# Hymba-style decoder layer on one core: start bytes of the split weights and of the activation blocks in SBUF

## The chip, the core and the metric

One NeuronCore of one Trainium2 chip runs the whole layer in one launch. The metric is device time in microseconds of that core, from runs of the whole program. Five engines work side by side: TensorE (PE: matmuls, with the weight loads listed apart as PEld), VectorE (DVE), ScalarE (ACT), GpSimd (POOL) and SyncE (SP, which here only issues DMAs). Data lies in SBUF, a memory of 128 partitions; each tile is a stretch of bytes at the same place in every partition, so one start byte says where it is. Matmul results go to PSUM.

## The reference

One decoder layer over 16 meta tokens and 512 tokens, width 2048, hidden width 5632, in float32. `l` is the only layer.

```python
h = jnp.concatenate([meta, x], axis=1)
n = _rmsnorm(h, g_mix[l])
q, k, v, gb, gc, u = jnp.split(n @ w_in[l], ...)
o_attn = _stick_breaking_attention(norm(q), norm(k), v)   # 8 heads of 128
o_conv = gb * _causal_dwconv(gc * u, conv_w[l])           # 1024 channels
o = jnp.concatenate([_rmsnorm(o_attn, g_attn_out[l]), _rmsnorm(o_conv, g_conv_out[l])], axis=-1)
h = h + o @ w_out[l]
n2 = _rmsnorm(h, g_ffn[l])
h = h + (jax.nn.silu(n2 @ w_gate[l]) * (n2 @ w_up[l])) @ w_down[l]
return h[:, N_META:]
```

## The kernel before

**Precision.** TensorE multiplies in a float32 form of lower precision (`F32R`). To keep float32 accuracy every operand is split in two: `hi` is the value rounded to `F32R` (a copy on ScalarE), `lo` the rest (a subtraction on VectorE). A product is three matmuls per tile of 128 rows: weight hi × activation hi, weight hi × activation lo, weight lo × activation hi.

**Stages.** The input projections and attention heads come first, then the short convolution (`pc`, `pu`, `pb` are its products; its activations are the tiles `nh` and `nl`, its weights `whi` and `wlo`), then the output projection, which works with `wide_product` on 512 columns. These use the helper at lines 161 to 173 or lines 639 to 648. From about 850 us on the feed-forward part runs: 44 pairs of gate and up products, then, over four chunks of the hidden width, 32 pairs of down products. Nearly all of its time is in `pair_product` (line 663).

**A pair.** `pair_product` multiplies a 2 × 2 arrangement of weight quarters with a 2 × 2 arrangement of activation halves with seven block products instead of eight. Seven activation blocks, `acts[0]` to `acts[6]`, stand against seven weight combinations, formed from the four loaded quarters `b11`, `b12`, `b21`, `b22` by sums on VectorE (`t1`, `t2`, `t3`, line 598). `block_product` (line 650) runs one of the seven: for each weight tile `k` of 128 columns the three matmuls at lines 659, 660 and 661, each of 128 × 128 weights with 256 activation columns. A block has 24 matmuls in a gate/up pair (8 weight tiles), and 15 or 18 in a down pair (5 or 6). Results gather in the PSUM banks `x`, `y`, `z`.

**The split weights.** `split_quad` (line 588) writes hi and lo of one weight combination into one tile of tag `s`, hi first, lo 4096 bytes behind it; ScalarE writes hi (line 591), VectorE lo (line 592). There are three such buffers, taken in turn. `prepare_ahead` keeps two combinations ahead of TensorE. As a pair takes seven of the three buffers' turns, every activation block meets each of the three in turn from pair to pair. The same buffers serve the output projection before (30 splits).

**The activation blocks.** `slot` (line 699) allocates a tile a little larger than the block and returns a view that starts 16 bytes in: hi and lo of `n` tiles of 256 columns, each tile 1024 bytes. In the gate/up stage the seven are `f0` to `f6`, which stay for the whole stage. In the down stage twelve tiles `r0` to `r11` form a ring: `load_acts` (line 845) loads the seven blocks of the next chunk into the next free ones from DRAM, by DMAs that GpSimd issues (line 851), while the chunk before is multiplied.

**Where the tiles lie.** Pools are stacks, so a tile's start follows from the sizes of those allocated before it. Modulo 128, in bytes, for the view that TensorE reads:

| | start byte modulo 128 |
|---|---|
| split weights, all three buffers, hi and lo | 96 |
| `f0`, `f2`, `f5` | 112 |
| `f1`, `f3`, `f4`, `f6` | 48 |
| ring tiles `r0`, `r2`, `r4`, `r7`, `r9`, `r11` | 112 |
| ring tiles `r1`, `r3`, `r5`, `r6`, `r8`, `r10` | 48 |
| `whi` and `wlo` of the convolution stage | 96 |
| `nh` as read by `pc` and `pu` (two halves of 258 columns) | 16 and 24 |
| `nl` as read by `pc` and `pu` | 80 and 88 |

The steps inside a block (1024 bytes from tile to tile of the activations, 512 of the weights, whole kilobytes from hi to lo) keep these remainders.

Of the kernel before, what the change touches and what calls it, by code (L numbers as in the profile page):

```python
# [10 lines left out]
F32R = mybir.dt.float32r  # L11
# [4 lines left out]
P = 128  # L16
# [9 lines left out]
T2 = SEQ // 2  # L26
# [6 lines left out]
def hybrid_layer(ctx: ExitStack, tc: tile.TileContext, xT, w_in, w_out, w_gu, w_down, vecs, out):  # L33
# [12 lines left out]
    def open_pool(name, bufs=1, **kw):  # L46
        return tc.alloc_tile_pool(name=name, bufs=bufs, reuse_waits="tile", **kw)
# [501 lines left out]
    sw = open_pool("sw", side="right")  # L549
# [12 lines left out]
    quads, sums, split_w, used = {}, {}, [], [0]  # L562
    S_AHEAD = 2
# [22 lines left out]
            load_quad(0, q)  # L586

    def split_quad(src, n):
        t = sw.tile([P, 2, 8 * P], F32R, tag="s", bufs=S_AHEAD + 1, name=f"s{len(split_w)}")
        hi, lo = (t[:, i, : n * P] for i in range(2))  # L590
        sc.copy(hi, src)  # L591
        ve.tensor_tensor(lo, src, hi.bitcast(F32), ALU.subtract)  # L592
        split_w.append((hi, lo))
# [6 lines left out]
    def prepare_pair():  # L600
        if len(split_w) < WIDE:
            with tc.high_priority():
                split_quad(wide[len(split_w)], 8)
                load_wide()
            return
# [4 lines left out]
        with tc.high_priority():  # L610
            b = {q: quads[i, q] for q in ("11", "12", "21", "22") if (i, q) in quads}
            if s == 0:
                split_quad(b["11"], n)
                add_quads(i, "t1", b["11"], b["12"])
                load_quad(i + 1, "11")
            elif s == 1:
                split_quad(sums["t1"], n)
                add_quads(i, "t2", sums["t1"], b["22"])
                add_quads(i, "t3", b["12"], b["22"])
                load_quad(i + 1, "12")  # L620
            elif s == 2:
                split_quad(sums["t2"], n)
            elif s == 3:
                split_quad(b["22"], n)
                load_quad(i + 1, "22")
            elif s == 4:
                split_quad(sums["t3"], n)
            elif s == 5:
                split_quad(b["21"], n)
                ve.tensor_tensor(sums["t2"], sums["t2"], b["21"], ALU.add)  # L630
                load_quad(i + 1, "21")
            else:
                split_quad(sums["t2"], n)
# [64 lines left out]

    def slot(pool, dt, n, tag, name):

        t = pool.tile([P, 2 * n * T2 + 16], dt, tag=tag, name=name)
        return t[:, 4 : 4 + 2 * n * T2].rearrange("p (a k t) -> p a k t", a=2, k=n)

    def pad(pool):
        pool.tile([P, 8], F32, name=f"pad_{pool.name}")

    acts = [slot(fpool, F32R, 8, f"f{i}", f"f{i}") for i in range(4)]
    fx = [dram.tile([P, 2, 8, T2], F32R, name=f"fx{s}") for s in range(4, 7)]
    for _ in range(4):
# [12 lines left out]
    for i, j in enumerate(OUT_TILES):  # L722
# [8 lines left out]
        half, k = divmod(j, 8)  # L731
# [22 lines left out]
        if i == KT - 1:  # L754
# [10 lines left out]
            def ring_tile(dt, name):  # L765
                i = n_ring[0] % 12
                n_ring[0] += 1
                return slot(rings_p[0 if i == 0 else 1 if i < 6 else 2], dt, 6, f"r{i}", name)

            r0 = ring_tile(F32R, "r0_0")  # L770
            fpool_last = open_pool("fpool_last")
            acts += [slot(fpool_last, F32R, 8, f"f{s}", f"f{s}") for s in range(4, 7)]
            for s in range(3):
                n = 7 if s else 8
# [40 lines left out]
    at = [(c, k) for c, n in enumerate(CHUNKS) for k in range(n)]  # L815
# [156 lines left out]
```

## Time and profile before

| | us |
|---|---|
| median of three runs | 2156.65 |
| the three runs | 2154.67 to 2163.67 |
| the profiled execution | 2159.77 |
| its span, first to last instruction | 2157.9 |

The granted TensorE clock over the span is 0.996 of full speed. In the profile an engine's line gives busy time, share of the span and the number of instructions. A matmul's duration runs from its start to its end, and matmuls overlap, so the time that a row of them takes is seen in the distance of their starts, or in how many start in a window. Rows of groups name line, engine, operation, output from inputs (buffer numbers left out), shape and count; then busy us and mean ns of one, then the idle time before them. Names in the profile leave numbers out: `f` stands for all of `f0` to `f6`, `s` for all three buffers, `r` for the ring.

### The profile page before, as it was taken

What the parts mean: (1) busy time and instruction counts of PE and PEld (TensorE: products, weight loads), DVE (VectorE), ACT (ScalarE), POOL (GpSimd) and SP (SyncE); (2) the same over time, 40 slices, a digit from 0 to 9 for tenths busy, and PEclk for the clock granted to TensorE, in tenths of its full rate; (3) what the DMA queues carried; (4) which work ended last, traced back from release to release, by engine and by line L of the source; (5) the groups of instructions that cost most, each with busy time, mean ns of one, the idle gap of its engine ahead of it and who ended that gap; (6) DMA issues with size and microseconds to landing.
All of it is one profiled execution on the core that took longest, in us unless ns stands there. A gap on an engine that the chain in (4) does not pass through costs nothing.

```text
span 2157.9 us, 39367 instructions
## 1 busy us (share of the span) xinstructions
PE 2118.5 (98%) x16086; PEld 2038.7 (94%) x16086; DVE 1645.9 (76%) x2137; ACT 1018.6 (47%) x1576; POOL 451.2 (21%) x579
## 2 busy tenths in 40 slices
PE   8999999999999998999999999999999899999999
PEld 7999999999988878999999999999999899999999
DVE  8777777433347677888888889889888677777798
ACT  6666565322224334454455445445544444444443
POOL 4111111101014541221211211212101323121222
PEclk9999999999999999999999999999999999999999
DMA  5222222222236656556555654655555999788863
GB/s 169 79 79 79 79 69 79 88 97 89 94 122 186 185 158 204 170 171 179 176 167 152 186 158 149 185 160 156 163 152 159 283 262 298 172 235 232 232 184 114
DMA packets 145941, 342.48 MB, mean 159 GB/s; under 512 B 13392, under 2 KB 58960, under 8 KB 145760
## 3 DMA queue, kind: packets, MB, share of 16 engines
q1 hardware_dynamic: 67680, 214.07, 31.6%
q0 software_dynamic: 78080, 125.89, 21.4%
q8 instruction: 126, 2.06, 0.4%
q14 instruction: 55, 0.45, 0.1%
HBM read 268.60 MB, written 71.30 MB: 158 GB/s over the span
## 4 chain that ended last, share of the span: by engine, by line
PE 90%; DMA 4%; DVE 3%; issue 1%; ACT 1%; POOL 1%; SPq 0%; DVEq 0%; POOLq 0%; ACTq 0%
PE x L659 11%; PE x L660 11%; PE x L661 11%; PE z L659 5%; PE z L660 5%; PE z L661 5%; PE y L661 3%; PE y L659 3%; PE y L660 3%; DMA b<-w_down 2%; PE po L645 2%; PE po L647 2%; PE po L646 2%; PE pv L166 1%; PE pu L170 1%; PE pc L170 1%
## 5 line engine op out<-in xcount | busy, mean ns | idle before, releaser
L591 ACT CAST s<-t 128x1024 fp32r<-128x1024 f32 (+2 forms) x304 | 285.5, 939 | 426.4 <-PE z L661 145.7
L592 DVE TENSOR_TENSOR s<-t,s 128x1024 fp32r<-128x1024 f32 (+2 forms) x304 | 343.7, 1130 | 114.8 <-ACT s L591 114.0
L659 PE MATMUL x<-f,s 128*128 128x256 f32 x1408 | 396.1, 281 | 3.4 <-DVE u L686 3.4
L660 PE MATMUL x<-f,s 128*128 128x256 f32 x1408 | 395.6, 281 | 0.0
L661 PE MATMUL x<-f,s 128*128 128x256 f32 x1408 | 395.3, 281 | 0.0
L591 ACT CAST s<-b 128x1024 fp32r<-128x1024 f32 (+2 forms) x228 | 214.0, 939 | 253.6 <-PE x L661 243.1
L659 PEld LDWEIGHTS x<-f,s 128*128 128x128 f32 x1408 | 266.7, 189 | 3.9 <-DVE u L686 3.6
L660 PEld LDWEIGHTS x<-f,s 128*128 128x128 f32 x1408 | 266.7, 189 | 0.0
L661 PEld LDWEIGHTS x<-f,s 128*128 128x128 f32 x1408 | 266.5, 189 | 0.0
L592 DVE TENSOR_TENSOR s<-b,s 128x1024 fp32r<-128x1024 f32 (+2 forms) x228 | 247.6, 1086 | 7.9 <-ACT s L591 5.9
L135 DVE TENSOR_TENSOR wlo<-raw,whi 128x512 fp32r<-128x512 f32 (+1 forms) x198 | 142.3, 720 | 130.9 <-ACT whi L134 130.3
L823 POOL DMA_DIRECT2D fd<-s x154 | 107.0, 890 | 643.7 <-DVE s L181 641.5
L134 ACT CAST whi<-raw 128x512 fp32r<-128x512 f32 (+1 forms) x198 | 121.3, 614 | 185.3 <-PE pu L168 65.5
L659 PE MATMUL x<-r,s 128*128 128x256 f32 x704 | 199.1, 283 | 9.4 <-DVE d L686 4.2
L659 PE MATMUL z<-f,s 128*128 128x256 f32 x704 | 199.0, 283 | 4.2 <-DVE w L739 2.2
L660 PE MATMUL z<-f,s 128*128 128x256 f32 x704 | 198.9, 283 | 2.4 <-DVE f L181 2.4
L660 PE MATMUL x<-r,s 128*128 128x256 f32 x704 | 198.3, 282 | 2.7 <-DMA r<-fd 2.7
L661 PE MATMUL z<-f,s 128*128 128x256 f32 x704 | 198.7, 282 | 0.0
L661 PE MATMUL x<-r,s 128*128 128x256 f32 x704 | 198.0, 281 | 0.4 <-DVE s L592 0.4
L598 DVE TENSOR_TENSOR t<-b,b 128x1024 f32<-128x1024 f32 (+2 forms) x152 | 164.7, 1083 | 27.5 <-DMA b<-w_down 19.9
L659 PEld LDWEIGHTS x<-r,s 128*128 128x128 f32 x704 | 133.1, 189 | 11.6 <-issue 6.7
L659 PEld LDWEIGHTS z<-f,s 128*128 128x128 f32 x704 | 133.0, 189 | 5.4 <-issue 2.3
(326 smaller groups left out, 5603.7 us busy)
## 6 DMA issues: line engine op xcount, KB each, us to landing
b<-w_gu SPq DMA_DIRECT2D x176, 512.0 KB, 3.5
raw<-w_in SPq DMA_DIRECT2D x92, 512.0 KB, 3.3
fd<-s POOLq DMA_DIRECT2D x154, 256.0 KB, 5.2
b<-w_down SPq DMA_DIRECT2D x64, 384.0 KB, 4.0
r<-fd POOLq DMA_DIRECT2D x28, 768.0 KB, 11.9
b<-w_down SPq DMA_DIRECT2D x64, 320.0 KB, 4.6
r<-fd POOLq DMA_DIRECT2D x28, 640.0 KB, 10.8
wide<-w_out SPq DMA_DIRECT2D x30, 512.0 KB, 3.9
```

Source lines behind the costliest of these rows:

```text
L134: sc.copy(hi[:, :c], raw)
L135: ve.tensor_tensor(lo[:, :c], raw, hi[:, :c].bitcast(F32), ALU.subtract)
L170: pe.matmul(ps, wl, ah[:, a:b], start=False, stop=k == last)
L591: sc.copy(hi, src)
L592: ve.tensor_tensor(lo, src, hi.bitcast(F32), ALU.subtract)
L598: ve.tensor_tensor(sums[name], a, b, ALU.add)
L645: pe.matmul(ps, hi[:, kk], ah, start=k == 0, stop=False)
L646: pe.matmul(ps, hi[:, kk], al, start=False, stop=False)
L659: pe.matmul(ps, hi[:, kk], act[:, 0, k], start=start and k == 0, stop=False, skip_group_check=not start)
L660: pe.matmul(ps, hi[:, kk], act[:, 1, k], start=False, stop=False, skip_group_check=not start)
L661: pe.matmul(ps, lo[:, kk], act[:, 0, k], start=False, stop=k == n - 1, skip_group_check=not start)
L823: gp.dma_start(fd[c][s][:, :, k], t[:, :, i])
```

## The change

Two allocations change. A split-weight tile is 128 bytes longer, and its view starts 32, 48 or 80 bytes in (8, 12 or 20 elements of 4 bytes), by the number of the split modulo 3, that is by buffer. An activation slot is 64 bytes longer than before, and its view starts 0, 16, 32, 48, 80, 96 or 112 bytes in, by the number in its tag modulo 7; so each of `f0` to `f6` has an offset of its own, and the twelve ring tiles go through the list once and start it again.

```diff
     def split_quad(src, n):
-        t = sw.tile([P, 2, 8 * P], F32R, tag="s", bufs=S_AHEAD + 1, name=f"s{len(split_w)}")
-        hi, lo = (t[:, i, : n * P] for i in range(2))
+        t = sw.tile([P, 16 * P + 32], F32R, tag="s", bufs=S_AHEAD + 1, name=f"s{len(split_w)}")
+        at = (8, 12, 20)[len(split_w) % 3]
+        hi, lo = (t[:, at + i * 8 * P :][:, : n * P] for i in range(2))
         sc.copy(hi, src)
         ve.tensor_tensor(lo, src, hi.bitcast(F32), ALU.subtract)
...
     def slot(pool, dt, n, tag, name):
 
-        t = pool.tile([P, 2 * n * T2 + 16], dt, tag=tag, name=name)
-        return t[:, 4 : 4 + 2 * n * T2].rearrange("p (a k t) -> p a k t", a=2, k=n)
+        t = pool.tile([P, 2 * n * T2 + 32], dt, tag=tag, name=name)
+        at = (0, 4, 8, 12, 20, 24, 28)[int(tag[1:]) % 7]
+        return t[:, at : at + 2 * n * T2].rearrange("p (a k t) -> p a k t", a=2, k=n)
```

With the new sizes every slot and every split tile starts at 96 modulo 128, so the views start here:

| | start byte modulo 128 |
|---|---|
| split weights, the three buffers | 0, 16, 48 |
| `f0` to `f6` | 96, 112, 0, 16, 48, 64, 80 |
| `r0` to `r6` | 96, 112, 0, 16, 48, 64, 80 |
| `r7` to `r11` | 96, 112, 0, 16, 48 |

The instructions of every engine and their order stay as they are. Tiles around the slots move by some hundred bytes and keep their remainder modulo 128, but for `d1` and `d2` of the down stage, which go from 32 to 96.

## The prediction

> **What bounds the kernel now.** I read the page first, then the whole run in stretches of 100 us, then single activation blocks, then the waits of TensorE.
>
> ```profile
> span 2157.9 us, 39367 instructions
> PE 2118.5 (98%) x16086; PEld 2038.7 (94%) x16086; DVE 1645.9 (76%) x2137; ACT 1018.6 (47%) x1576; POOL 451.2 (21%) x579
> PEclk9999999999999999999999999999999999999999
> PE 90%; DMA 4%; DVE 3%; issue 1%; ACT 1%; POOL 1%; SPq 0%; DVEq 0%; POOLq 0%; ACTq 0%
> ```
>
> TensorE carries 90% of the chain that ends last, at full granted clock. So the time is a number of matmuls times the step from one start to the next, and an address can matter only by that step or by making another engine late enough to stop TensorE.
>
> ```profile
> 900.00:1000.00 100.00, 100.00 (x847) 99.84 (x846) 89.09 (x97) 49.75 (x65) 21.56 (x28) 1.00 0.58 170
> ...
> 1500.00:1600.00 100.00, 100.00 (x849) 100.00 (x848) 87.74 (x99) 49.63 (x66) 13.16 (x19) 1.00 0.54 156
> ```
>
> Columns: busy us and count of TensorE, weight loads, VectorE, ScalarE, GpSimd; granted clock; DMA share; GB/s. In the gate/up stage 847 matmuls of 256 columns start in 100 us, 118.0 ns apart, and TensorE never stops. Now one gate/up pair, cut at the starts of its seven blocks f0 to f6 (24 matmuls each; the bracketed count includes matmuls that reach over an edge, so divide the length by 24):
>
> ```profile
> 1295.78:1298.63 2.85, 2.85 (x27) 1.00 0.29 101
> 1298.63:1301.50 2.87, 2.87 (x27) 1.00 0.25 93
> 1301.50:1304.22 2.72, 2.72 (x26) 1.00 0.60 191
> 1304.22:1307.08 2.86, 2.86 (x26) 1.00 0.03 7
> 1307.08:1309.92 2.84, 2.84 (x27) 1.00 0.64 125
> 1309.92:1312.77 2.85, 2.85 (x26) 1.00 1.09 310
> 1312.77:1315.63 2.86, 2.86 (x26) 1.00 1.28 390
> ```
>
> Same work seven times, but f2 takes 2.72 us (113.3 ns a matmul) and the other six 17.13 us together (119.0 ns). TensorE waits for nothing in either, and DMA goes from 7 to 390 GB/s without an effect. Longer steps show inside the matmuls:
>
> ```profile
> L660 PE MATMUL x<-f,s 128*128 128x256 f32 x7 | 1.9, 276 | 0.0
> L660 PE MATMUL z<-f,s 128*128 128x256 f32 x8 | 2.3, 282 | 0.0
> ```
>
> The first row is f2, the second f3 beside it: 6 ns longer for the same shape. So something slows the matmul itself by some 5 ns in most blocks and by nothing in a few. That is what operand addresses could change.
>
> **Which addresses.** While a matmul streams its block, the weights of the next one are loaded; I compare the two start bytes modulo 128. Before the change weights always start at 96. Blocks start at 112 (f0, f2, f5: the same 64-byte half as the weights, "near") or 48 (f1, f3, f4, f6: the other half, "far"). From the windows above, near is (2.85 + 2.72 + 2.85) / 72 = 116.9 ns, far (2.87 + 2.86 + 2.84 + 2.86) / 96 = 119.1 ns. Another stage, whose weights also start at 96, has activations at 16 and 24 (nh, far) or 80 and 88 (nl, near):
>
> ```profile
> L166 PE MATMUL pc<-nh,whi 128*128 128x258 f32 x256 | 51.7, 284 | 0.0
> L168 PE MATMUL pc<-nl,whi 128*128 128x258 f32 x256 | 51.5, 282 | 0.0
> ```
>
> Near is again 2 ns shorter, with other tiles and offsets. But near does not make a block free: f0 and f5 cost nearly what far blocks cost. In the down stage two ring tiles that both start at 112 differ too, and each repeats itself:
>
> ```profile
> 1969.26:1970.96 1.70, 1.70 (x18) 1.00 0.66 175
> 1981.68:1983.38 1.70, 1.70 (x18) 1.00 0.85 228
> 2064.03:2066.17 2.14, 2.14 (x20) 1.00 0.51 191
> 2078.99:2081.13 2.14, 2.14 (x21) 1.00 0.50 187
> ```
>
> 15 matmuls in 1.70 us are 113.3 ns, 18 in 2.14 us are 118.9 ns, with the same start modulo 128. So near blocks have at least two rhythms, a free one and a slow one, and which one a block falls into is settled by something that the start byte alone does not tell. No far block of the pair runs free.
>
> **The change, part by part.**
>
> *Instructions.* None is added, removed or reordered on any engine; one GpSimd load of h_over waits for one semaphore less. Term: 0.
>
> *Near and far shares.* There are 11,088 matmuls of 256 columns (44 gate/up pairs × 7 blocks × 24, and 16 down pairs each × 7 × 15 and × 7 × 18). Before, 3 of 7 blocks and 6 of 12 ring tiles are near: 5,040. After, weights start at 0, 16 or 48 in turn and blocks at 96, 112, 0, 16, 48, 64, 80. I call a difference (block minus weights, modulo 128) of 96, 112, 0 or 16 near, since 112, 120 and 16 are near by the rows above, and 32 to 80 far, since 48, 56 and 80 are; the edges at 96, 0, 32 and 64 are an assumption. Counted over all matmuls, 5,608 are then near. 568 more × 2.2 ns (119.1 − 116.9) = −1.2 us. If only the absolute half decides, 5,041 are in the weights' half and the term is 0. I take −1.2.
>
> *Rhythm.* Addresses move by other amounts than 128 bytes too, so each block may fall into another rhythm. f2 gains 24 × (119.0 − 113.3) = 0.137 us a pair, 6.0 us over 44 pairs. Losing that with nothing in its place costs +6.0 us. All near blocks in the free rhythm: f2's 1,056 are so already, the other 4,552 × 5.7 ns = −25.9 us. I take 0, the same share as now, since nothing tells which block locks where.
>
> *Weights 16 bytes off a 32-byte border.* After, two of three split buffers start at 16 or 48; before, all at 96. No weight load of the trace does that. Below: 0, as with activations: f blocks (off by 16) cost 118.0 ns on average. Above: the nearest worse alignment, the halves that start at 24 and 88, 8 bytes off:
>
> ```profile
> 439.78 0.40 PE L168 MATMUL pu<-nl,whi 128*128 128x258 f32 x2
> ...
> 442.19 0.28 PE L170 MATMUL pu<-nh,wlo 128*128 128x258 f32 x1
> ```
>
> 20 matmuls, half of them 8 bytes off, in 2.41 us: 120.5 ns, against 118.0 plus 0.8 for two more columns. That is 1.7 ns on average, 3.4 ns if the odd half bears it. On two thirds of 11,088, 7,392 × 3.4 = +25 us. I take 0, since an offset of 16 is nearer to the blocks that have it than to an offset of 8.
>
> *Writers.* ScalarE and VectorE write the split weights at the new offsets. They already write f blocks 16 bytes off and st tiles on the border:
>
> ```profile
> L180 ACT CAST f<-src 128x256 fp32r<-128x256 f32 x34 | 12.2, 399 | 4.0 <-DVE src L751 3.1 <-DVE src L749 0.9
> L180 ACT CAST st<-src 128x256 fp32r<-128x256 f32 x8 | 3.2, 402 | 0.0
> ```
>
> 399 against 402 ns on ScalarE; on VectorE, in a stretch without GpSimd work,
>
> ```profile
> L181 DVE TENSOR_TENSOR f<-src,f 128x256 fp32r<-128x256 f32 x3 | 1.1, 413 | 0.0
> L181 DVE TENSOR_TENSOR st<-src,st 128x256 fp32r<-128x256 f32 x8 | 3.3, 414 | 0.0
> ```
>
> No difference: 0. The cover would matter if I am wrong, for VectorE is 89% busy in the gate/up stage, with 11 us spare in 100.
>
> *Ring loads.* They land at other offsets. TensorE's waits for them in the down stage:
>
> ```profile
> PE x L660 <- DMA r<-fd: 2.7, 3, 1.3
> PE x L659 <- DMA r<-fd: 1.9, 2, 1.6
> PE z L660 <- DMA r<-fd: 1.6, 1, 1.6
> PE y L659 <- DMA r<-fd: 0.4, 1, 0.4
> PE z L659 <- DMA r<-fd: 0.2, 1, 0.2
> ```
>
> 6.8 us in all, the most that could go; doubled, +6.8. I take 0, as the bytes are the same.
>
> *Sum.* The profiled execution took 2159.77 us, 1.87 around its span of 2157.9; 2159.77 − 1.2 = 2158.6. The median of the runs is 2156.65, 3.1 below that execution, so the forecast is 2155.4, written 2155.
>
> The trace has the same shape at 276 and 282 ns without a wait. The Trainium skill (SBUF — State Buffer, "Who interferes with whom") says that on the engine side only the port pair of VectorE and GpSimd causes contention and that TensorE and ScalarE never wait on anyone. By that rule no offset moves the time; 276 against 282 ns speaks against it, though not which partner it is. By the rule the sum would be 2157, by the rows 2155.
>
> **The rivals.**
>
> *The offsets change nothing.* The two rhythms come from when a block starts, not from where it lies. For it: r tiles with one start byte at 113.3 and 118.9. Against it: f2 and the 258-column rows. Time: 2157.
>
> *More blocks run free.* Now some 1 in 5 near matmuls does (f2's 1,056 of 5,040). If weights and blocks at many different offsets meet freely in 3 of 5, that is 3,365 of 5,608, 2,309 more × 5.7 = −13.2, with −1.2: 2142; all near blocks free: 2129.5. For it: the free rhythm occurs and holds for whole blocks. Against it: with three weight offsets each block meets a new difference from pair to pair, so a rhythm cannot settle.
>
> *Weight loads 16 bytes off cost.* Slower: place, the load of each next weight tile from two of three split buffers; price up to 3.4 ns on 7,392 matmuls, +25 − 1.2: 2180. It makes the kernel slower by over 0.5% from (10.8 + 1.2) / 7,392 = 1.6 ns; at 2.5 ns it gives 2174. For it: an offset of 8 does cost on the other operand. Against it: the blocks at 16 already.
>
> **How the numbers follow.** A change of 0.5% (10.8 us) is about what a measurement of this kernel can tell from no change. Forecast (same within 0.5%, small shift) 0.33; offsets change nothing 0.12; more blocks free 0.34; costly weight loads 0.21. Of the free case 0.32 is beyond −10.8 us and 0.02 within; of the slow case 0.19 beyond and 0.02 within: faster 0.32, same 0.49, slower 0.19. The range goes from 2131 (nearly all near blocks free) to 2173 (loads at 2.4 ns), leaving out about 2 in 10; the forecast's own range is 2148 to 2164, the loss or gain of one f block's rhythm and a little.
>
> **What would show it.** Counts of matmuls in 100 us stay at 845 to 853 by the forecast, over 855 in the free case, under 840 in the slow one. Windows on single f blocks: f3 (near with all three weight offsets after the change) below f6 (far with all three). Weight-load and matmul durations by split buffer would show the third rival: every third load shorter. Splits on ScalarE at 1053 ns and VectorE at 1231 to 1263 ns unchanged shows the writers right:
>
> ```profile
> L591 ACT CAST s<-t 128x1024 fp32r<-128x1024 f32 x176 | 185.3, 1053 | 271.7 <-PE z L661 112.8 <-PE x L661 82.3 <-PE y L661 76.7
> L592 DVE TENSOR_TENSOR s<-b,s 128x1024 fp32r<-128x1024 f32 x132 | 162.5, 1231 | 2.7 <-ACT s L591 2.5
> L592 DVE TENSOR_TENSOR s<-t,s 128x1024 fp32r<-128x1024 f32 x176 | 222.3, 1263 | 68.5 <-ACT s L591 68.5
> ```
>
> Wrong altogether: new waits of TensorE, or a step that far and near blocks share but that differs from 116 to 119 ns.

## The result, and the profile after

| | before | after |
|---|---|---|
| median of 18 runs of each | 2160.48 us | 2165.07 us |
| lowest and highest | 2154.67 to 2163.67 | 2160.48 to 2168.44 |
| profiled execution | 2159.77 | 2168.44 |

The ratio is 1.0025, with a 95% interval of 1.0017 to 1.0033: some 5 us slower, within the half per cent that was called no change. The forecast was a gain of 1.2 us. So the time lies in the range, but the sum had the wrong sign, and the terms below show why. It also lies 1 us above the forecast's own range, 2148 to 2164. Of the 9.7 us between the forecast and the median, 3.8 are the base: three runs of before had the median 2156.65, the 18 here have 2160.48.

The page of the kernel after first: span, busy time with counts, granted clock in 40 slices, and the chain of waits by engine.

```profile
span 2166.5 us, 39367 instructions
PE 2128.8 (98%) x16086; PEld 2047.2 (94%) x16086; DVE 1647.0 (76%) x2137; ACT 1020.2 (47%) x1576; POOL 452.2 (21%) x579
PEclk9999999999999999999999999999999999999999
PE 91%; DMA 4%; DVE 3%; issue 1%; POOL 1%; ACT 1%; SPq 0%; DVEq 0%; POOLq 0%; ACTq 0%
```

The instructions are the same 39,367, the matmuls the same 16,086, and TensorE still carries the chain. VectorE, ScalarE and GpSimd are busy within 1.6 us of before. TensorE is busy 10.3 us longer for the same work, so the time went into the step of the matmuls, or into their clock.

Stretches of before (length; then busy us and count of TensorE, weight loads, VectorE, ScalarE, GpSimd; granted clock, DMA share, GB/s):

```profile
0.00:850.00 850.00, 830.55 (x5266) 756.43 (x5266) 541.74 (x847) 392.73 (x681) 178.66 (x241) 0.99 0.36 115
850.00:1680.00 830.00, 829.97 (x7016) 828.93 (x7015) 733.12 (x797) 412.96 (x544) 150.43 (x197) 1.00 0.56 164
1680.00:1800.00 120.00, 110.84 (x907) 107.83 (x907) 87.41 (x122) 53.71 (x95) 35.89 (x47) 1.00 0.94 270
1800.00:2170.00 370.00, 347.16 (x2904) 345.52 (x2902) 283.66 (x372) 159.23 (x258) 86.26 (x94) 0.99 0.72 204
```

The same stretches of after:

```profile
0.00:850.00 850.00, 833.38 (x5240) 756.26 (x5241) 538.90 (x846) 390.36 (x677) 178.96 (x241) 0.99 0.36 115
850.00:1680.00 830.00, 829.96 (x7010) 829.55 (x7010) 732.57 (x796) 414.25 (x543) 150.85 (x197) 1.00 0.56 164
1680.00:1800.00 120.00, 109.69 (x876) 106.97 (x875) 84.74 (x120) 52.35 (x90) 32.22 (x42) 0.97 0.89 257
1800.00:2170.00 370.00, 355.78 (x2967) 354.40 (x2966) 290.74 (x379) 163.22 (x266) 90.14 (x99) 0.99 0.74 209
```

By 1680 us before has started 12,282 matmuls and after 12,250: 32 × 118 ns = 3.8 us of delay, of which 26 arose ahead of 850 us. There, and not in the feed-forward part, lies most of it. Another 31 (3.7 us) are lost from 1680 to 1800 us, where the granted clock is 0.97 against 1.00. The clock varies between executions of one kernel: of the 18 runs of after, the two at a mean of 0.997 took 2160.48 and 2162.82 us, those at 0.991 and 0.992 took 2167.73 and 2168.38. That is the likely reason, though not shown for these two, why the profiled executions are 8.7 us apart and the medians only 4.6.

Ahead of 850 us is the output projection. Of its 720 matmuls of 512 columns 711 follow each other without a pause, so one window holds 711 steps. Before, then after:

```profile
640.49:803.24 162.75, 162.75 (x713) 133.53 (x711) 113.84 (x151) 62.93 (x105) 77.33 (x81) 1.00 0.58 173
```

```profile
641.21:807.36 166.15, 166.15 (x713) 133.74 (x711) 114.07 (x151) 63.85 (x105) 77.91 (x81) 1.00 0.57 171
```

162.75 / 711 = 228.9 ns, and 166.15 / 711 = 233.7 ns: 4.8 ns more for the same matmuls at full clock, 3.4 us in all. These matmuls read the same split buffers, whose starts the change moved. The prediction did not count them.

For every kernel below I took the steps in this way from the trace: distances from one matmul's start to the next, those over 145 ns (270 ns for 512 columns) left out as waits or half clock.

| step in ns | before | after | × matmuls | us |
|---|---|---|---|---|
| output projection, 512 columns | 228.9 | 233.7 | 720 | +3.4 |
| gate/up blocks, 256 columns | 118.13 | 118.33 | 7,392 | +1.5 |
| down blocks, 256 columns | 118.30 | 118.42 | 3,696 | +0.4 |

The sum, 5.3 us, lies within the interval of the measured difference (3.7 to 7.1 us). It leaves out waits and half clock.

### The profile page after: what moved, and what is told of

It is laid out like the page before. It is cut to its first block, busy times and chain, and to the rows that moved or that the text cites. A ratio compares the mean times of both kernels' runs of the same rounds, so it can differ in the third digit from the quotient of the medians.

```text
span 2166.5 us, 39367 instructions
## 1 busy us (share of the span) xinstructions
PE 2128.8 (98%) x16086; PEld 2047.2 (94%) x16086; DVE 1647.0 (76%) x2137; ACT 1020.2 (47%) x1576; POOL 452.2 (21%) x579
## 4 chain that ended last, share of the span: by engine, by line
PE 91%; DMA 4%; DVE 3%; issue 1%; POOL 1%; ACT 1%; SPq 0%; DVEq 0%; POOLq 0%; ACTq 0%
PE x L660 11%; PE x L661 11%; PE x L662 11%; PE z L661 5%; PE z L662 5%; PE z L660 5%; PE y L661 3%; PE y L662 3%; PE y L660 3%; PE po L648 2%; PE po L646 2%; PE po L647 2%; DMA b<-w_down 2%; PE pv L166 1%; PE pu L170 1%; PE pc L170 1%
## 5 line engine op out<-in xcount | busy, mean ns | idle before, releaser
L599 DVE TENSOR_TENSOR t<-b,b 128x1024 f32<-128x1024 f32 (+2 forms) x152 | 164.7, 1083 | 25.4 <-DMA b<-w_down 18.9
```

Of the source, the lines that this page charges most:

```text
L599: ve.tensor_tensor(sums[name], a, b, ALU.add)
```

## The experiments

**The theory** that came out of the comparison: the step of a matmul hangs on the difference of the start bytes of its activations and its weights, modulo 256. The rival is the prediction's own rule, by differences modulo 128, with 96 to 16 near and cheap and 32 to 80 far and dear; a further rival is that the start byte of one operand counts by itself. Below, a difference is always activations minus weights.

The steps that the runs showed, with the ratio to before (f: gate/up blocks, r: down blocks; differences modulo 256):

| | difference of f and r blocks | projection ns | f ns | r ns | ratio (95%) |
|---|---|---|---|---|---|
| before | 4 values | 228.9 | 118.13 | 118.30 | |
| after | 16 values | 233.7 | 118.33 | 118.42 | 1.0025 [1.0017, 1.0033] |
| e1 | 12 values | 233.7 | 117.75 | 118.03 | 1.0003 [0.9994, 1.0013] |
| e2 | 9 values | 228.9 | 118.30 | 118.56 | 1.0017 [1.0009, 1.0026] |
| e3 | as after | 232.6 | 118.32 | 118.39 | 1.0016 [1.0007, 1.0025] |
| e4 | 64, 192 | 232.6 | 116.24 | 115.77 | 0.9931 [0.9918, 0.9943] |
| e5 | 192 | 228.9 | 116.49 | 116.47 | 0.9934 [0.992, 0.9948] |
| e6 | 96 | 228.9 | 119.99 | 119.98 | 1.0084 [1.0071, 1.0098] |
| e7 | 192 | 233.4 | 115.28 | 117.05 | 0.9925 [0.9898, 0.9953] |
| e8 | 448 (= 192) | 228.9 | 116.26 | 116.30 | 0.9919 [0.9887, 0.995] |
| e9 | as before | 233.3 | 118.17 | 118.27 | 1.0009 [0.9999, 1.002] |
| e10 | 192; f0, r0, r6 at 64 | 228.9 | 115.27 | 116.12 | 0.9914 [0.9897, 0.993] |
| e11 | 192; f0, r0, r6 at 96 | 228.9 | 116.13 | 115.17 | 0.9888 [0.9855, 0.9921] |
| e12 | 192, one split later | 228.9 | 113.37 | 116.43 | 0.9877 [0.9832, 0.9923] |

### The two halves of the change, one at a time

e1 takes the edit of `split_quad` alone, e2 that of `slot` alone.

> Only the split weights move (0, 16, 48); activation slots stay as before (112 and 48). If the loss sits in the output projection, because its weights no longer start at 96, its 720 matmuls of 512 columns step 233 to 234 ns instead of 229 (+3.4 us) and the kernel is 3 to 6 us slower than before. If the activation offsets make the loss, it is within 1 us of before.

> Only the activation slots move; split weights stay at 96. If the loss sits in the output projection's weights, its matmuls stay at 229 ns and the kernel is within 2 us of before, whatever the rhythms of the 256-column blocks add or take. If the activation offsets make the loss (by slower blocks, or by ring loads that land later and more half-clock stretches), it is 4 to 6 us slower.

The projection's window in e1:

```profile
640.61:806.75 166.14, 166.14 (x712) 133.73 (x711) 115.06 (x153) 64.39 (x105) 78.11 (x81) 1.00 0.57 171
```

It is that of after; e2 has 228.9 ns again. So the projection's 3.4 us belong to the split weights. By the table e1 loses these 3.4 us and wins 2.8 + 1.0 us in the blocks, in sum −0.4: no difference, as measured. e2 loses 1.3 + 1.0 us; measured are 1.9 to 5.6. So neither expectation came out whole: e1 was to be 3 to 6 us slower and is not, and e2 was to be within 2 us and is 1.9 to 5.6 slower, of which the steps of its blocks give 2.3. No part of the change costs what the prediction's third rival feared: e1 has two of three weight buffers 16 bytes off, and its blocks are faster. By buffer, f and r together, the two at 16 and 48 step 118.0 and 119.0 ns in after and 118.6 and 117.1 in e1, the one at 0 118.1 and 117.8: no common sign.

### The projection's splits back at offset 0

```diff
-        at = (8, 12, 20)[len(split_w) % 3]
+        at = (8, 12, 20)[len(split_w) % 3] if len(split_w) >= WIDE else 0
```

> The changed kernel, but the 30 splits of the output projection start at 96 as before. If the projection carries the loss, 3.4 us of the 4.6 come back: at most 1.5 us slower than before. If not, it stays 4 to 5 us slower.

A miss. The projection took

```profile
640.80:806.20 165.40, 165.40 (x713) 133.53 (x711) 113.88 (x151) 63.67 (x105) 77.78 (x81) 1.00 0.57 171
```

or 232.6 ns, and not 228.9. The splits were back at 96 modulo 128, but a tile is 128 bytes longer than before, so the three buffers start at 96, 224 and 352 modulo 512, where before all three start at 480. Against activations at 32 the differences are 192, 64 and 192 modulo 256 (before: 64), with 233.1, 231.5 and 233.3 ns. So the remainder modulo 128, on which the prediction rested, doesn't tell the step; and 64 among other differences is not 64 throughout, so what runs beside it counts too. e9 measures the same term cleanly. The f blocks, which this edit leaves alone, repeat those of after to 0.01 ns in the mean: in this arrangement the rhythm of a block is not chance, but follows the addresses.

### One start for all blocks

e4 puts all slots at 80 and the gate, up and down splits at 16 modulo 128, on the sizes of the changed kernel, which leaves the differences 64 and 192 modulo 256.

```diff
-        at = (8, 12, 20)[len(split_w) % 3]
+        at = 12 if len(split_w) >= WIDE else 0
...
-        at = (0, 4, 8, 12, 20, 24, 28)[int(tag[1:]) % 7]
+        at = 28
```

> Every activation slot starts at 80 and every feed-forward split at 16, the pair that stepped 113.3 ns in all 15 blocks where f6 met it; output projection at 96. If the two start bytes modulo 128 settle the rhythm, all 11,088 matmuls step 113.3 ns: some 55 us faster than before (ratio near 0.975). If the block's place in the order or its higher address settles it, f6 may stay fast and the others scatter between 113 and 121 ns: within 12 us of before.

Blocks at 192 stepped 114.3 ns in the mean, blocks at 64 117.8. By the prediction's rule both are far (64 modulo 128) and should have cost 119. This is the first version that beats before, by 0.7%.

### A single difference: 192, 96, and 192 in two other ways

e5 and e6 keep the weights where they are before (480 modulo 512) and give every block the same start, by slots without an offset and pads between the pools:

```diff
-        t = pool.tile([P, 2 * n * T2 + 16], dt, tag=tag, name=name)
-        return t[:, 4 : 4 + 2 * n * T2].rearrange("p (a k t) -> p a k t", a=2, k=n)
+        t = pool.tile([P, 2 * n * T2], dt, tag=tag, name=name)
+        return t.rearrange("p (a k t) -> p a k t", a=2, k=n)
...
     def pad(pool):
-        pool.tile([P, 8], F32, name=f"pad_{pool.name}")
+        n = dict(fpool=80, fpool_last=0, ring_0=56, ring_a=80, ring_b=0)[pool.name]
+        if n:
+            pool.tile([P, n], F32, name=f"pad_{pool.name}")
```

These are the pads of e5 (blocks at 160); e6 has 104, 0, 32, 104, 0 (blocks at 64).

> Split weights as before (all start at 480 modulo 512); every activation block starts at 160, so block minus weights is 192 modulo 512 in all 11,088 matmuls. If that difference modulo 512 sets the rhythm, every block steps 113.3 to 113.9 ns, as all blocks with that difference did so far, which is 4.5 to 4.9 ns less than before: 50 to 54 us less work on TensorE, 40 to 54 us off the time if the down stage's loads keep up (ratio 0.975 to 0.982). If the order of the blocks or other address bits set it, the mean stays at 116 to 119 ns and the time within 20 us of before. Output projection at 229 ns as before.

> The same with every block at 64: block minus weights 96 modulo 512 everywhere, the difference whose blocks stepped 119.9 to 120.0 ns so far. By the difference: every block at 120 ns, 1.8 ns more than before, about 20 us slower (ratio 1.008 to 1.01). By the 64-byte-half rule of the prediction this difference was counted as near and would give 117 ns, some 13 us faster. By the order of the blocks: within 5 us of before.

The 100 us windows of e6:

```profile
1000.00:1100.00 100.00, 100.00 (x835) 100.00 (x835) 87.54 (x94) 48.51 (x65) 19.59 (x26) 1.00 0.59 174
1500.00:1600.00 100.00, 100.00 (x836) 100.00 (x835) 87.02 (x96) 49.41 (x65) 13.16 (x19) 1.00 0.52 150
```

835 and 836 where before has 847 and 849. By the table the blocks step 120.0 ns in the gate/up stage and in the down stage, and the kernel is 0.8% slower. 96 is near by the prediction's rule, which gives 117 ns. That rule is refuted, and so is the rival that offsets change nothing: e5 and e6 have the same instructions and differ in the sizes of three pads.

Neither e4 nor e5 reached 113.3 ns in all blocks, which would have won 11,088 × 4.9 = 54 us; they won 15 and 14. Windows of single f blocks of e5, of 24 matmuls, in the order of time:

```profile
1190.26:1192.98 2.72, 2.72 (x27) 2.72 (x25) 2.44 (x3) 1.32 (x2) 1.24 (x1) 1.00 0.84 262
1192.98:1195.70 2.72, 2.72 (x27) 2.72 (x25) 2.72 (x3) 1.95 (x3) 1.57 (x2) 1.00 0.52 200
1195.70:1198.83 3.13, 2.88 (x27) 2.69 (x25) 3.10 (x4) 2.00 (x4) 0.00 (x0) 1.00 0.47 130
1198.83:1201.76 2.93, 2.93 (x24) 2.93 (x25) 2.93 (x4) 1.17 (x2) 1.41 (x2) 1.00 0.50 160
1201.76:1204.59 2.83, 2.83 (x27) 2.83 (x25) 1.98 (x4) 1.05 (x1) 0.00 (x0) 1.00 1.02 276
1210.24:1213.07 2.83, 2.83 (x27) 2.83 (x25) 2.44 (x3) 1.32 (x2) 0.00 (x0) 1.00 0.29 82
```

Two rhythms at one and the same difference: 2.72 / 24 = 113.3 ns, and from the fifth row on 2.83 / 24 = 117.8. Each holds for 14 blocks or more. Between them stands the 3.13 us of the third row, of which TensorE was busy only 2.88.

The other two versions test the difference itself. e7 moves weights (to 448) and blocks (to 128) by 32 bytes; e8 puts the blocks at 416, a difference of 448.

```diff
     acc_h = hpool.tile([P, SEQ], F32, name="acc_h")
+    hpool.tile([P, 8], F32, name="pad_h")
...
-        n = dict(fpool=80, fpool_last=0, ring_0=56, ring_a=80, ring_b=0)[pool.name]
+        n = dict(fpool=80, fpool_last=0, ring_0=48, ring_a=80, ring_b=0)[pool.name]
```

This is e7 against e5; e8 is e5 with pads 16, 0, 120, 16, 0.

> As e5_diff_192, but weights and blocks both start 32 bytes lower (448 and 128): the difference stays 192. If only the difference counts, blocks step as there, 113.3 to 113.9 ns. If the absolute start counts, they scatter. The output projection's activations do not move, so its difference goes from 64 to 96: if its rhythm too hangs on the difference, its 720 matmuls leave 229 ns.

> Block minus weights 448 everywhere (192 plus 256). Blocks with that difference stepped 113.3 to 114.5 ns so far, but f5 of the changed kernel 117.5. If the pattern repeats every 256 bytes, it is as fast as e5_diff_192; if every 512, up to 1 ns a matmul (11 us) slower than that one, and still 35 to 50 us faster than before.

Both have the same two rhythms, 113.3 and 117.8 ns, and no third, and the same time as e5. So for 192 the difference counts, and it counts modulo 256. That it is not modulo 128 rests on e4, where 64 and 192 step differently among each other; no run has all blocks at 64. How the blocks share out over the two rhythms differs (e7 has 57% of its f blocks at 113.3, e8 34%). In e7 the projection, whose activations stayed, went from 228.9 to 233.4 ns as its difference went from 64 to 96.

The difference doesn't fix the step alone. In before, f2 and f5 both lie at 144 modulo 256 (400 and 144 modulo 512) and step 113.8 and 118.6 ns. As in e3, what stands beside a block counts too, or the address beyond 256; the runs don't separate these two.

### Before, with weights and blocks moved together

```diff
     acc_h = hpool.tile([P, SEQ], F32, name="acc_h")
+    hpool.tile([P, 8], F32, name="pad_h")
...
             rings_p = [open_pool("ring_0")]
-            pad(rings_p[0])
```

> The kernel before, with the split weights and all activation blocks moved by the same 32 bytes, so that every block keeps its difference to the weights; only the projection's activations stay, so its difference goes from 64 to 96 modulo 256. If the difference alone sets the step: f and r blocks keep 118.1 and 118.3 ns and their pattern block by block, the projection goes from 228.9 to 233.3 ns, 720 x 4.4 = 3.2 us, ratio 1.0015. If the absolute start of weights or blocks counts: other f and r steps, some block over 0.5 ns away. If the projection is hidden behind something: ratio 1.000 with the longer projection.

```profile
641.04:806.94 165.90, 165.90 (x713) 133.46 (x711) 113.88 (x151) 63.72 (x105) 77.61 (x81) 1.00 0.57 171
```

The projection takes 3.15 us more than before over 711 matmuls; f and r stay within 0.04 ns, and the single blocks f0 to f6 repeat those of before within 0.15 ns, f2 and f5 with theirs. The trace is as the difference has it. The time is not told apart: 1.0009 holds both the expected 1.0015 and, just, no change.

### What holds a rhythm, and what switches it

e10 and e11 place f0, r0 and r6 at another difference than the rest, to see what one block hands to the next.

```diff
-        t = pool.tile([P, 2 * n * T2], dt, tag=tag, name=name)
-        return t.rearrange("p (a k t) -> p a k t", a=2, k=n)
+        more = 32 if tag in ('f0', 'r0', 'r6') else 0
+        t = pool.tile([P, 2 * n * T2 + more], dt, tag=tag, name=name)
+        return t[:, 0 : 2 * n * T2].rearrange("p (a k t) -> p a k t", a=2, k=n)
```

This is e10 against e5, with ring_0 and ring_b at 24 and 96; e11 has 24 for 32, and 32 and 104.

> All blocks at difference 192 as in the version that had two rhythms (113.3 and 117.75 ns), except f0, r0 and r6, which lie at 64 (their step so far 118.4 ns). If the rhythm is a phase that a block hands to the next one, and a block at 64 hands on the phase of 113.3 (as 192 behind 64 mostly had in the version with four differences), the other blocks run at 113.3 and the mean is (6 x 113.3 + 118.4) / 7 = 114.0 ns: 11,088 x 4.1 = -45 us against before, ratio 0.979. If the phase is redrawn at each block or by something outside the matmuls, the two rhythms stay mixed as at 192 throughout: 116.5 ns, ratio 0.993. If 64 hands on the phase of 117.75: 117.8 ns, ratio 0.998.

> As the version with f0, r0 and r6 at difference 64, but these three at 96, where every block so far stepped 120.0 ns and had no second rhythm; the others stay at 192. At 64 the phase was only handed through (113.3 stayed 113.3, 117.75 stayed 117.75) and was redrawn where TensorE waited. If a block at 96 sets the phase, the six blocks behind it always take the same rhythm: all at 113.3, mean (6 x 113.3 + 120.0) / 7 = 114.3 ns, 11,088 x 3.9 = -43 us, ratio 0.980; or all at 117.75, mean 118.1 ns, ratio 1.000. If 96 also only hands the phase through, the two stay mixed: about 117 ns, ratio 0.994.

Neither sets the rhythm; both mostly hand it through. Comparing f6 ahead of f0 with f1 behind it, over 42 pairs each: in e10 27 went from 113.3 to 113.3, 12 from 117.8 to 117.8 and 3 from 117.8 to 113.3; in e11 21, 20 and 1. None went from 113.3 to 117.8. Neither wins the 43 to 45 us that a set rhythm would have given. By the table their medians are below e5's because more blocks stood in the faster rhythm; that share varies between executions, and the interval of e10 overlaps that of e5.

What does switch it is in e5's third row. TensorE at its end, then ScalarE in the same 3 us (start, duration, engine and line, operation; in brackets the idle time ahead and who ended it):

```profile
1198.31 0.28 PE L661 MATMUL x<-f,s 128*128 128x256 f32 x1
1198.83 0.39 PE L659 MATMUL z<-f,s 128*128 128x256 f32 x1 [0.25 <-ACT p L678]
```

```profile
1195.90 1.06 ACT L591 CAST s<-t 128x1024 fp32r<-128x1024 f32 x1 [0.46 <-PE z L661]
1197.88 0.62 ACT L180 CAST s<-even 128x512 fp32r<-128x512 f32 x1 [0.93 <-DVE even L838]
1198.41 0.37 ACT L678 COPY p<-z 128x256 f32<-128x256 f32 x1
```

The fourth block adds into the bank `z`, which ScalarE must have copied out (`p`, line 678). That copy stands on ScalarE behind the split of the gated block (`s<-even`, line 180), which waits 0.93 us for VectorE. So TensorE pauses 0.25 us, and comes out of the pause in the other rhythm. Not each such pause switches it, but in the three versions at 192 throughout nothing else does: from 860 to 1680 us such a pause, seen as a distance of over 145 ns between the third and the fourth block, stands 9 times in e5 and 10 times each in e7 and e8. The f blocks change between 113.3 and 117.8 ns at 7, 5 and 6 of them, in both directions, and at no other place. e12 hands that split on to after the copy:

```diff
-            store_acts(even_f[:, 0:2], 2, (0, 4), f // 2)
+            late[0] = lambda: store_acts(even_f[:, 0:2], 2, (0, 4), f // 2)
...
-        x = pair_product(acts, g1, u1, None if f else h_scale)
+        x = pair_product(acts, g1, u1, h_scale if not f else late[0] if f % 2 else None)
```

> All blocks at difference 192, and the split of the gated block handed on to after the copy of the next pair's z (p from L678 is issued on ScalarE ahead of the split s from L180, not behind it). In the version without this, each change between 113.3 and 117.75 ns in the gate/up stage that was looked at stood at the fourth block of a pair, where TensorE waited 0.2 us for that copy. If the wait is what switches the rhythm: none of these waits and no switch behind 900 us of the profile, all f blocks in one rhythm; at 113.3 this is 7,392 x 4.8 = -35 us, with the r blocks as before this edit (-7) -42 in all, ratio 0.980; at 117.75 it is -3 and -7, ratio 0.995. If the rhythm switches by itself: several switches as before, about 116.5 ns, ratio 0.993. If the handed-on split comes too late for the store and the loads behind it: new waits in the stage, ratio above 0.995.

From 850 to 1650 us of e12:

```profile
850.00:1650.00 800.00, 800.00 (x7061) 800.00 (x7060) 734.22 (x802) 415.66 (x548) 149.40 (x203) 1.00 0.58 172
```

TensorE is busy for all of the 800 us, and 800 / 7061 = 113.3 ns: one rhythm, not one switch. The median is the lowest of all, 2124.66 us against 2160.12, though the interval of its ratio overlaps that of e11. Of its six runs four lie at 2120 to 2126 us and two at 2147.75 and 2150.45, near the expectation's two cases (0.980 and 0.995 of 2160 are 2117 and 2149). That the two ran at 117.8 throughout fits, but they were not profiled. So the runs show that without the pause nothing switched; what chooses the rhythm at the start of the stage stays open.

## Why the prediction was off

Two steps failed: the rule of near and far, and a sum that left the output projection out.

**Instructions: right.** Counts on all engines are the same.

**"Near and far shares" (−1.2 us): the step that failed.** The prediction sorted differences modulo 128 into a cheap and a dear half. After the change the near matmuls of the gate/up stage step 118.7 ns and the far ones 118.0: the order is turned round. It had named the test itself, f3 (near with all three weights) below f6 (far with all three). f3 and f6 in three pairs that follow each other, f3 first each time:

```profile
1208.29:1211.12 2.83, 2.83 (x26) 2.83 (x25) 2.54 (x3) 1.32 (x2) 1.42 (x2) 1.00 0.48 127
1216.79:1219.53 2.74, 2.74 (x27) 2.74 (x26) 1.85 (x3) 1.05 (x1) 0.00 (x0) 1.00 0.63 197
1228.02:1230.89 2.87, 2.87 (x27) 2.87 (x26) 2.84 (x4) 1.51 (x3) 0.00 (x0) 1.00 0.00 0
1236.53:1239.37 2.84, 2.84 (x27) 2.84 (x26) 1.95 (x3) 1.05 (x1) 0.00 (x0) 1.00 1.26 376
1248.02:1250.87 2.85, 2.85 (x27) 2.85 (x26) 2.85 (x3) 1.32 (x2) 1.41 (x2) 1.00 0.52 158
1256.54:1259.41 2.87, 2.87 (x27) 2.87 (x25) 1.98 (x3) 1.05 (x1) 0.00 (x0) 1.00 0.58 183
```

f3 takes 8.55 us, f6 8.45. The far block at 2.74 has the difference 192 modulo 256, that of e5. In before the near half was cheap only because of f2: without its 113.8 ns near is the mean of f0 and f5, 118.6. One block in a fast rhythm was read as a rule, and the 258-column rows, 2 ns apart, seemed to bear it out. (By the start bytes of the built kernel 5,613 matmuls are near after the change, not 5,608; the term would be −1.3.) The counts in 100 us, 847 from 1000 to 1100 and 848 from 1500 to 1600, stayed at the 845 to 853 of the forecast, so that sign could not tell.

**The output projection: not in the sum.** The prediction counted the 11,088 matmuls of 256 columns and passed over 720 of 512 columns that read the same three buffers. Their term is +3.4 us, the largest of all. It was to be had beforehand, at least as an unknown: the bound that a gate/up block gave (some 5 ns) on 720 matmuls is 3.6 us.

**"Rhythm" (0, from −25.9 to +6.0): right in kind.** f2 did lose its fast rhythm, 113.8 to 120.5 ns, which over 1,056 matmuls is 7.0 us. The other six won 0.2 to 1.9 ns each, 5.4 us together. The two nearly cancel, as the prediction guessed without a reason: that was luck. The shares and the rhythm can't be told apart in the steps. Together they were put at −1.2 us and came to +1.9 (1.5 in gate/up, 0.4 in down). The lower end was real, but for another arrangement of addresses: e12 wins 35 us.

**"Weights 16 bytes off" (0, to +25 us): right,** by e1. **"Writers" (0): right,** for the splits take 1050 ns on ScalarE and 1232 to 1270 on VectorE, against 1053 and 1231 to 1263:

```profile
L592 ACT CAST s<-t 128x1024 fp32r<-128x1024 f32 x176 | 184.7, 1050 | 266.7 <-PE z L662 110.1 <-PE x L662 80.4 <-PE y L662 76.2
```

```profile
L593 DVE TENSOR_TENSOR s<-t,s 128x1024 fp32r<-128x1024 f32 x176 | 223.5, 1270 | 67.7 <-ACT s L592 67.3
L593 DVE TENSOR_TENSOR s<-b,s 128x1024 fp32r<-128x1024 f32 x132 | 162.6, 1232 | 2.1 <-ACT s L592 2.1
```

**"Ring loads" (0): right.** TensorE's waits for them, from 1680 to 1800 us:

```profile
PE x L660 <- DMA r<-fd: 3.5, 1, 3.5
PE z L661 <- DMA r<-fd: 1.9, 1, 1.9
...
PE x L661 <- DMA r<-fd: 1.2, 1, 1.2
...
PE y L660 <- DMA r<-fd: 0.4, 1, 0.4
```

7.0 us where there were 6.8.

**The rivals.** "The offsets change nothing" is refuted by e5 and e6. "More blocks run free" did not happen in this change. The reason that the prediction gave against it, three weight offsets that keep a rhythm from settling, isn't borne out: in e2 each f block keeps one difference, and none runs free (116.8 to 119.6 ns), while f6 in after steps 114.1 ns each of the 15 times that it meets the buffer at difference 192. With one good difference for all (e5, e8) it does happen, for part of the blocks. "Costly weight loads" is refuted.

**The page's rule.** The Trainium skill (SBUF — State Buffer, "Who interferes with whom") lists two independent read ports for TensorE, one for the moving operand and one for weight loads, and says that TensorE never waits on anyone. e6's blocks hold 120.0 ns whether DMA moves 150 or 174 GB/s, and e5, with the same instructions on every engine, has no f block at that step; that far no run shows TensorE's step waiting on another engine. But with independent reads the difference of the two starts should not matter, and it moves the step from 113.3 to 120.0 ns. What inside the chip couples them, no run here shows.

## What to carry to other kernels

Where TensorE is the bound and a matmul of 256 columns steps slower than the best block beside it, look at the start bytes of activations and weights: their difference modulo 256 is worth up to 6% of the step, and pads of some tens of bytes set it. Give all blocks one difference that has a fast rhythm (192 here), rather than many different ones, and then remove the short waits of TensorE, since each may change the rhythm of all the blocks behind it. Run such a kernel several times: two of e12's six runs were 1.2% slower than the rest. All of this was measured at 128 × 128 weights and float32 in its reduced form, for 256 columns, and for 512 only as far as the projection goes. Before a price per matmul goes into a sum, list all matmuls that read the moved tiles, with their shapes.

## What the hardware showed that was not expected

- **Steps in steps.** The stable rhythms at a single difference are 113.3, 117.8 and 120.0 ns: 17, 17⅔ and 18 times 6.67 ns.
- **A wait of 0.25 us has an effect that is larger than itself.** The one above is followed by blocks that are 0.11 us longer each. In the profiled executions e5's f blocks average 116.5 ns and e12's 113.4, which is 7,392 × 3.1 = 23 us; the listed waits for that copy from 850 to 1680 us come to 0.7 us in e5.
- **Not all of a faster step arrives.** e4 and e5 win 20.7 and 18.9 us by the steps of the table, and 14 to 15 us in the time. TensorE's listed waits behind 860 us come to 18.1 us in e5 and 15.8 in before; what else takes the rest was not followed up.
- **Stretches at half clock** (granted clock 0.5). They add up to 17.1 us of the span in the profiled execution of before, 27.3 in that of after, and 31.6 in that of e1, which took 2159.36 us against 2159.77 of before. They come and go from run to run and, by that, are not put down to the change.
